# Moving the start of the split-weight tiles by 0, 32, 64 or 96 bytes from one tile to the next

## The chip, the cores and the metric

The kernel runs on one core of one Trainium2 chip. The metric is the device time of one execution in microseconds; 2619.27 us is the median of three runs of the kernel before (2615.98 to 2622.2). The profiled execution, from which all rows below come, took 2616.97 us; its span from the first to the last instruction is 2614.9 us.

## The reference

One hybrid decoder layer for 512 tokens of width 2048, in float32. Cut to what matters here:

```
n1   = rms_norm(x);  proj = n1 @ w_in                      # 2048 x (1024 + 3072 + 1024 + 16 + 4096)
y_pool = causal_pool_mixer(...);  o = gated_delta_rule(...)  # 8 heads, chunks along the sequence
merged = sigmoid(gate_pool) * (y_pool @ w_up_pool) + sigmoid(gate_dn) * (y_dn @ w_up_dn)
h    = x + merged @ w_out                                  # 2048 x 2048
h    = h + hierarchical_moe(rms_norm(h))                   # 32 experts, top 2 of one group
h    = h + sigmoid(rms_norm(h) @ w_ple_gate) * (p @ w_ple_proj)   # w_ple_gate 2048 x 2048
out  = rms_norm(h)
```

The large products outside the experts (w_in, w_up_pool, w_up_dn, w_out, w_ple_gate) are what the change is about.

## The kernel before, in words

**The split.** A large product is made of three passes in the format fp32r. Each operand is split in two: a high part (`hi`, ScalarE casts it, line 94) and a low part (`lo` = raw minus high, VectorE, line 95). `mm3` (lines 97 to 101) then issues three matmuls into the same PSUM bank: high by high (L99), and the two mixed products (L100, L101). A profile shows for each of them a MATMUL on PE (the moving operand streams through, 512 or 256 columns) and an LDWEIGHTS on PEld (the stationary operand, 128 columns, loaded while the matmul before it runs). A row names the tiles in the order moving, stationary.

**Weights in the mixer.** `load_w` (L322) brings 512 KB of a weight by DMA into `raw` (three buffers), splits it into `whi` and `wlo` (two buffers each), and one such tile feeds 24 matmuls (`proj`, L373: four slices of the contraction, two halves of the columns, three passes). There the weight slice is stationary and the activations (`n1h`, `n1l`; later `yd`, `yh`, `yl`) move. `next_w` (L358) asks for the next tile when it hands one out, so ScalarE and VectorE split one tile ahead. The first four weight tiles are split elsewhere, into `fhi` and `flo` (L241), with 256 moving columns, and the 16 columns of beta and alpha into `ba_h` and `ba_l` (`gates_ba`, L489).

**Output projection.** In `project_out` (L879) it is the other way round: the weights of w_out (`whi`, `wlo`, 512 columns) move, and 128-column slices of the split activations `mh` and `ml` (three buffers each, `parts`, L886) are stationary. A weight tile again feeds 24 matmuls, an activation tile 12. While the last block runs, `h` is transposed for the router (L915 copies the result, L919 multiplies by the router's weights).

**Tail.** The gate of the per-layer embedding: `gate_weights` (L1523) splits w_ple_gate into `whi` and `wlo` of a second pool (four buffers each); they move, with 512 columns in three blocks and 256 in the last two (`tail`, L1532), and slices of `xh` and `xl` are stationary.

The experts between output projection and tail multiply whole float32 tiles (`wm` by `xe`, `hmT`) with 64 stationary columns, and a few fp32r tiles of their own (`G` by `ghi`, `yhi` by `GT`).

**Where the tiles lie.** A pool lays the buffers of its tiles end to end in each partition. In the built program the starts of the fp32r operands are these, modulo 256 bytes (slices of an operand start at multiples of 512 bytes from there, those of `ba_h` and `ba_l` at multiples of 64):

| product | moving starts at | stationary starts at |
|---|---|---|
| mixer (n1, yd, yh, d by whi, wlo) | 224 | 224 |
| first tiles (n1 by fhi, flo) | 224 | 64 |
| beta and alpha (n1 by ba_h, ba_l) | 224 | 64, 128, 192, 0 in turn |
| output projection (whi, wlo by mh, ml) | 224 | 224 |
| tail (whi, wlo by xh, xl) | 160 | 128 |

**What sets the order.** Instructions are recorded as the code runs and put in order by a scheduler, per engine; in the norm and the experts TensorE's order (in the norm ScalarE's and VectorE's too) is the one in which the code is written. Each engine runs its own list in order.

Of the kernel before, what the change touches and what calls it, by code (L numbers as in the profile page):

```python
# [10 lines left out]
F32R = mybir.dt.float32r  # L11
# [6 lines left out]
P = 128  # L18
T = 512
# [43 lines left out]
class Layer:  # L63
    def __init__(self, ctx, tc, a, dbg=None):
        self.ctx, self.tc, self.nc, self.a, self.dbg = ctx, tc, tc.nc, a, dbg or {}
        self.consts = ctx.enter_context(tc.tile_pool(name="consts", bufs=1))
        self.psum = ctx.enter_context(tc.tile_pool(name="psum", bufs=4, space=bass.MemoryType.PSUM))

# [250 lines left out]
            self.xs.append(x)  # L319


    def load_w(self, src, width):  # L322
        nc = self.nc
        raw = self.p_w.tile([P, 1024], F32, name="raw", bufs=3)
        hi = self.p_w.tile([P, 1024], F32R, name="whi", bufs=2)
        lo = self.p_w.tile([P, 1024], F32R, name="wlo", bufs=2)
        r = raw.rearrange("p (k c) -> p k c", c=width)
        nc.sync.dma_start(r, src)
        self.last_split = self.split(hi, lo, raw)
        return hi.rearrange("p (k c) -> p k c", c=width), lo.rearrange("p (k c) -> p k c", c=width)  # L330
# [548 lines left out]
    def project_out(self, pp):  # L879
        nc, a = self.nc, self.a  # L880
        for t in range(NT):
            nc.scalar.dma_start(self.h[:, t, :], a["x"][0, t * P:(t + 1) * P, :])
        self.pl = self.bank("dl")
        self.ss2 = self.p_rt.tile([P, NT, 4], F32, name="ss2", bufs=1)

        def parts():  # L886
            for k in 4 * list(range(KD)):
                h = pp.tile([P, T], F32R, name="mh", bufs=3)
                l = pp.tile([P, T], F32R, name="ml", bufs=3)
                self.split(h, l, self.m[k])  # L890
                yield h, l

        parts = parts()
        ready = [next(parts)]
        for i, (c0, w) in enumerate(((0, 512), (512, 512), (1024, 512), (1536, 512))):
            cs = slice(c0, c0 + w)
            ps = [self.bank("mm") for _ in range(NT)]
            n = 1024 // w
            for k0 in range(0, KD, n):
                hi, lo = self.next_w()  # L900
                for k in range(n):
                    ready.append(next(parts, None))
                    mh, ml = ready.pop(0)
                    for t in range(NT):
                        s = slice(t * P, (t + 1) * P)
                        self.mm3(ps[t][:, 0:w], mh[:, s], ml[:, s], hi[:, k, :], lo[:, k, :],
                                 start=k0 + k == 0, stop=k0 + k == KD - 1)
            for t in range(NT):
                d = self.h[:, t, cs]
                nc.vector.scalar_tensor_tensor(d, ps[t][:, 0:w], 0.5, d, op0=OP.mult, op1=OP.add)  # L910
            for k in range(c0 // P, (c0 + w) // P):
                f = pp.tile([P, T], F32, name="hT", bufs=2)
                pt = self.h_transposed(k)
                if k % 2:
                    nc.vector.tensor_copy(f, pt)  # L915
                else:
                    nc.scalar.copy(f, pt)
                o = 64 * (k % 2)
                nc.tensor.matmul(self.pl[o:o + 36, :], self.wr[:, k, :], f, start=k < 2, stop=k >= KD - 2)  # L919
            for t in range(NT):  # L920
                j = pp.tile([P, T], BF16, name="sqj", bufs=1)
                nc.scalar.activation(j[:, 0:w], self.h[:, t, cs], AF.Square, accum_out=self.ss2[:, t, i:i + 1])
# [600 lines left out]
    def gate_weights(self, w):  # L1523

        raw = self.next_weights().rearrange("p k c -> p (k c)")
        for i in range(2):
            hi = self.p_w.tile([P, 1024], F32R, name="whi", bufs=4)
            lo = self.p_w.tile([P, 1024], F32R, name="wlo", bufs=4)
            self.split(hi, lo, raw[:, 1024 * i:1024 * i + 1024])
            yield hi.rearrange("p (k c) -> p k c", c=w), lo.rearrange("p (k c) -> p k c", c=w)  # L1530

# [175 lines left out]
```

## Time and profile before

| | us |
|---|---|
| median of 3 runs | 2619.27 |
| profiled execution | 2616.97 |
| its span | 2614.9 |
| PE busy in the span | 2511.0 |
| ScalarE (ACT) busy | 776.7 |
| VectorE (DVE) busy | 1148.9 |

The profile shows one execution. PE's busy time is that of pipelined matmuls and overlaps itself: a matmul of 512 columns is shown with some 390 ns, though the next one starts some 227 ns after it. What a matmul costs in a dense stretch is therefore read from the starts of successive matmuls in the timeline (start in us with two decimals), over as many as stand in one stretch. The granted clock of TensorE is 0.992 of full speed over the span; the mixer, the output projection's stretches cited below and the tail's cited stretches stand at 1.00, which is the 2.4 GHz level.

### The profile page before, as it was taken

The numbers are of one execution on the slowest core, as the hardware profiler recorded it, in microseconds if no ns is written. First come the engines' busy times: TensorE is split into PE (matmuls) and PEld (weight loads), VectorE is DVE, ScalarE is ACT, GpSimd is POOL, SyncE is SP. The second block draws the span as 40 slices with busy tenths as digits, with TensorE's granted clock in tenths as the row PEclk, the third lists the DMA queues.
The fourth block names the chain that finished last, engine by engine and source line by source line (L and its number), as shares of the span: only waits on it lengthen the run. The fifth ranks groups of instructions, "written<-read, shape, count | busy, mean of one in ns | idle before, by whom it ended". The sixth has DMA issues, their size and how long they took to land. (4 is left out here: it accounts for less than half of the span.)

```text
span 2614.9 us, 30940 instructions
## 1 busy us (share of the span) xinstructions
PE 2511.0 (96%) x12358; PEld 1720.5 (66%) x12358; DVE 1148.9 (44%) x2042; ACT 776.7 (30%) x1308; POOL 83.8 (3%) x92
## 2 busy tenths in 40 slices
PE   7999999999999999999989899999999999989998
PEld 6788888887888888877754444444444444444788
DVE  6475766765222233345453343333334333315435
ACT  4233242424222222234434222223222222113323
POOL 1001110100000000000000000000000000000001
PEclk9999999999999999999989999999999999999999
DMA  5222223234333333373237799999999999977222
GB/s 153 81 79 73 79 58 94 68 97 125 97 97 97 97 97 97 97 292 126 81 138 283 324 378 416 379 422 374 422 377 421 384 421 376 401 307 278 97 97 97
DMA packets 197975, 554.16 MB, mean 212 GB/s; under 512 B 30378, under 2 KB 127043, under 8 KB 148035
## 3 DMA queue, kind: packets, MB, share of 16 engines
q1 hardware_dynamic: 194610, 543.61, 55.4%
q10 hardware_dynamic: 2640, 4.33, 0.5%
q0 software_dynamic: 576, 4.19, 0.4%
q8 instruction: 99, 1.62, 0.2%
q14 instruction: 50, 0.40, 0.0%
HBM read 545.01 MB, written 7.08 MB: 211 GB/s over the span
## 5 line engine op out<-in xcount | busy, mean ns | idle before, releaser
L1138 PE MATMUL ps_mm<-wm,xe 128*64 128x512 f32 x2048 | 454.7, 597 | 10.6 <-DMA wm<-in_w_gate_dram 5.3
L99 PE MATMUL ps_mm<-n1h,whi 128*128 128x512 f32 x1120 | 450.4, 402 | 0.9 <-ACT whi L94 0.9
L101 PE MATMUL ps_mm<-n1h,wlo 128*128 128x512 f32 x1120 | 437.3, 391 | 1.7 <-DVE wlo L95 1.6
L100 PE MATMUL ps_mm<-n1l,whi 128*128 128x512 f32 x1120 | 437.1, 390 | 0.0
L95 DVE TENSOR_TENSOR wlo<-raw,whi 128x1024 fp32r<-128x1024 f32 x206 | 254.4, 1235 | 412.5 <-ACT whi L94 401.4
L94 ACT CAST whi<-raw 128x1024 fp32r<-128x1024 f32 x206 | 216.3, 1050 | 545.1 <-PE ps_mm L100 538.9
L1138 PEld LDWEIGHTS ps_mm<-wm,xe 128*64 128x64 f32 x2048 | 141.8, 137 | 287.0 <-issue 264.1
L95 DVE TENSOR_TENSOR glo<-h,ghi 128x512 fp32r<-128x512 f32 x128 | 137.2, 1096 | 361.1 <-ACT ghi L94 352.8
L94 ACT CAST ghi<-h 128x512 fp32r<-128x512 f32 x128 | 139.6, 1134 | 425.3 <-PE ps_dl L1113 314.2
L101 PEld LDWEIGHTS ps_mm<-n1h,wlo 128*128 128x128 f32 x1120 | 210.0, 188 | 47.3 <-DVE wlo L95 2.5
L99 PEld LDWEIGHTS ps_mm<-n1h,whi 128*128 128x128 f32 x1120 | 210.8, 188 | 40.3 <-ACT whi L94 1.3
L100 PEld LDWEIGHTS ps_mm<-n1l,whi 128*128 128x128 f32 x1120 | 210.9, 188 | 38.7
L1197 PE MATMUL ps_mm<-wm,hmT 128*64 128x512 f32 x960 | 218.8, 601 | 9.0 <-DVE eidx L1353 6.9
L1221 DVE TENSOR_TENSOR h<-h,ps_dl 128x512 f32<-128x512 f32 x256 | 160.2, 682 | 98.7 <-PE ps_dl L1219 95.9
L1197 PEld LDWEIGHTS ps_mm<-wm,hmT 128*64 128x64 f32 x960 | 66.5, 137 | 135.2 <-issue 130.0
L1113 PE MATMUL ps_dl<-G,ghi 128*128 128x256 f32 x512 | 134.2, 298 | 1.9 <-DVE G L1092 0.9
L1114 PE MATMUL ps_dl<-G,glo 128*128 128x256 f32 x512 | 128.5, 288 | 5.2 <-DVE glo L95 5.2
L1113 PEld LDWEIGHTS ps_dl<-G,ghi 128*128 128x128 f32 x512 | 99.2, 194 | 42.4 <-issue 38.9
L1218 PE MATMUL ps_dl<-yhi,GT 128*128 128x512 f32 x256 | 107.8, 421 | 14.0 <-ACT xe L1120 14.0
L1114 PEld LDWEIGHTS ps_dl<-G,glo 128*128 128x128 f32 x512 | 99.2, 194 | 7.1 <-DVE glo L95 6.9
L101 PE MATMUL ps_mm<-whi,ml 128*128 128x512 f32 x256 | 100.0, 391 | 2.1 <-DVE ml L95 2.1
L1219 PE MATMUL ps_dl<-ylo,GT 128*128 128x512 f32 x256 | 100.7, 393 | 0.0
(402 smaller groups left out, 3262.4 us busy)
## 6 DMA issues: line engine op xcount, KB each, us to landing
wm<-in_w_gate_dram SPq DMA_DIRECT2D x128, 1024.0 KB, 8.7
wm<-in_w_up_dram SPq DMA_DIRECT2D x128, 1024.0 KB, 10.2
wm<-in_w_down_dram SPq DMA_DIRECT2D x128, 1024.0 KB, 9.5
raw<-in_w_in_dram SPq DMA_DIRECT2D x144, 512.0 KB, 3.7
raw<-in_w_out_dram SPq DMA_DIRECT2D x32, 512.0 KB, 3.7
wm<-in_w_ple_gate_dram SPq DMA_DIRECT2D x16, 1024.0 KB, 5.0
raw<-in_w_up_dn_dram SPq DMA_DIRECT2D x16, 512.0 KB, 3.5
raw<-in_w_up_pool_dram SPq DMA_DIRECT2D x16, 512.0 KB, 3.6
```

The costliest lines, as they stand in the source:

```text
L94: i = self.nc.scalar.copy(hi, src)
L95: return i, self.nc.vector.tensor_tensor(lo, src, hi.bitcast(F32), op=OP.subtract)
L99: mm(ps, whi, xhi, start=start, stop=False)
L100: mm(ps, whi, xlo, start=False, stop=False)
L101: mm(ps, wlo, xhi, start=False, stop=stop)
L1113: nc.tensor.matmul(p, hi[:, t, :], Gf[:, t, :], start=t == 0, stop=False)
L1114: nc.tensor.matmul(p, lo[:, t, :], Gf[:, t, :], start=False, stop=t == NT - 1)
L1138: nc.tensor.matmul(ps[64 * i:64 * i + 64, :], xe[k][:, c0 + 64 * i:c0 + 64 * i + 64], ws[i][:, j, :], start=k == 0, stop=k == KD - 1)
L1197: nc.tensor.matmul(out[cb][64 * i:64 * i + 64, :], hT[:, k, 64 * i:64 * i + 64], ws[i][:, cb * T:(cb + 1) * T], start=k == 0, stop=k == 3)
L1218: nc.tensor.matmul(pc, GT[:, s], yh, start=True, stop=False)
L1219: nc.tensor.matmul(pc, GT[:, s], yl, start=False, stop=True)
L1221: nc.vector.tensor_tensor(d, d, pc, op=OP.add)
```

## The change

A helper `shifted` counts the tiles made under a name, allocates each 32 elements (128 bytes per partition) longer, and returns a view that begins 8 elements (32 bytes) further on after each full turn of the name's buffers: 0, 32, 64, 96 bytes, then 0 again. `whi`, `wlo`, `mh` and `ml` are taken from it; `raw`, the activations, `xh`, `xl` and everything else stay as they are.

```diff
+        self.turns = {}
...
+    def shifted(self, pool, name, n, bufs):
+
+        i = self.turns[name] = self.turns.get(name, -1) + 1
+        t = pool.tile([P, n + 32], F32R, name=name, bufs=bufs)
+        o = 8 * (i // bufs % 4)
+        return t[:, o:o + n]
+
     def load_w(self, src, width):
         nc = self.nc
         raw = self.p_w.tile([P, 1024], F32, name="raw", bufs=3)
-        hi = self.p_w.tile([P, 1024], F32R, name="whi", bufs=2)
-        lo = self.p_w.tile([P, 1024], F32R, name="wlo", bufs=2)
+        hi = self.shifted(self.p_w, "whi", 1024, 2)
+        lo = self.shifted(self.p_w, "wlo", 1024, 2)
...
             for k in 4 * list(range(KD)):
-                h = pp.tile([P, T], F32R, name="mh", bufs=3)
-                l = pp.tile([P, T], F32R, name="ml", bufs=3)
+                h = self.shifted(pp, "mh", T, 3)
+                l = self.shifted(pp, "ml", T, 3)
...
         for i in range(2):
-            hi = self.p_w.tile([P, 1024], F32R, name="whi", bufs=4)
-            lo = self.p_w.tile([P, 1024], F32R, name="wlo", bufs=4)
+            hi = self.shifted(self.p_w, "whi", 1024, 4)
+            lo = self.shifted(self.p_w, "wlo", 1024, 4)
```

Since each buffer is 128 bytes longer, the second buffer of a name also lies 128 bytes further on modulo 256. In the built program the stationary starts of the mixer are thus 224, 96, 0, 128, 32, 160, 64, 192 modulo 256 in turn, a new one with each tile, against a moving operand that stays at 224. In the output projection both operands take many pairs of starts; in the tail the moving one takes all eight multiples of 32 and the stationary one stays at 128.

The order of the instructions is the same on PE, ACT, POOL and SP. On DVE two instructions move, at the end of the output projection, where the last copies for the router (hT) meet the router's root of the mean square (rs2s, rsq_j, rsq_b) and a small constant (turn). DVE there in the kernel before:

```order
L910 SCALAR_TENSOR_TENSOR h<-ps_mm,h 128x512 x4
L915 COPY hT<-ps_dl 128x512
L935 TENSOR_REDUCE rs2s<-ss_8854 128x4
L936 TENSOR_SCALAR rs2s<-rs2s 128x4
L81 TENSOR_SCALAR rsq_j_10309<-rs2s 128x4
L84 TENSOR_TENSOR rsq_b_10310<-rsq_j_10309 128x4
```

In the changed kernel, where all lines below the helper are eight further on, the same place on DVE reads:

```order
L918 SCALAR_TENSOR_TENSOR h<-ps_mm,h 128x512 x4
L923 COPY hT<-ps_dl 128x512 x2
L943 TENSOR_REDUCE rs2s<-ss_8854 128x4
L1357 MEMSET turn 128x1
L944 TENSOR_SCALAR rs2s<-rs2s 128x4
L82 TENSOR_SCALAR rsq_j_10309<-rs2s 128x4
```

The last copy of hT, which stood after the seventh small instruction of the root, now stands ahead of all of them, and the constant `turn`, which stood behind the root, now stands behind its first instruction.

## Rows read from the trace of the kernel before

**Rows 1.** The page's busy times: busy us, share of the span, instructions.

```profile
PE 2511.0 (96%) x12358; PEld 1720.5 (66%) x12358; DVE 1148.9 (44%) x2042; ACT 776.7 (30%) x1308; POOL 83.8 (3%) x92
```

**Rows 2.** Groups: line, engine, op, out<-moving,stationary, count | busy us, mean ns | idle before.

```profile
L99 PE MATMUL ps_mm<-n1h,whi 128*128 128x512 f32 x1120 | 450.4, 402 | 0.9 <-ACT whi L94 0.9
L95 DVE TENSOR_TENSOR wlo<-raw,whi 128x1024 fp32r<-128x1024 f32 x206 | 254.4, 1235 | 412.5 <-ACT whi L94 401.4
L94 ACT CAST whi<-raw 128x1024 fp32r<-128x1024 f32 x206 | 216.3, 1050 | 545.1 <-PE ps_mm L100 538.9
L101 PE MATMUL ps_mm<-whi,ml 128*128 128x512 f32 x256 | 100.0, 391 | 2.1 <-DVE ml L95 2.1
L99 PE MATMUL ps_mm<-whi,xh 128*128 128x512 f32 x128 | 51.4, 401 | 0.0
L99 PE MATMUL ps_mm<-yd,whi 128*128 128x512 f32 x128 | 49.8, 389 | 0.0
L99 PE MATMUL ps_dl<-whi,xh 128*128 128x256 f32 x128 | 35.7, 279 | 0.0
L99 PE MATMUL ps_dl<-whi,xh 128*128 128x512 f32 x64 | 25.3, 395 | 0.0
```

**Rows 3.** Timeline of PE, output projection, 16 starts: start us, us, instruction.

```profile
1156.14 0.39 PE L100 MATMUL ps_mm<-wlo,mh 128*128 128x512 f32 x1
...
1159.54 0.39 PE L100 MATMUL ps_mm<-wlo,mh 128*128 128x512 f32 x1
```

**Rows 4.** Timeline of PE, tail with 512 columns, 12 starts.

```profile
2456.22 0.39 PE L101 MATMUL ps_mm<-whi,xl 128*128 128x512 f32 x1
...
2458.79 0.40 PE L100 MATMUL ps_mm<-wlo,xh 128*128 128x512 f32 x1
```

**Rows 5.** Timeline of PE, beta and alpha, 13 starts.

```profile
56.69 0.39 PE L99 MATMUL ps_mm<-n1h,ba_h 128*16 128x512 f32 x1
...
59.44 0.39 PE L99 MATMUL ps_mm<-n1h,whi 128*128 128x512 f32 x1
```

**Rows 6.** Tile ba_h: duration ns min/median/max, first and last start us.

```profile
L100 PE MATMUL ps_mm<-n1l,ba_h x16: 389/396/397, 56.9 to 71.3; 128*16 128x512 f32 x16
```

**Rows 7.** Timeline of PE, first tiles with 256 columns, 17 starts.

```profile
47.96 0.28 PE L99 MATMUL ps_mm<-n1h,fhi 128*128 128x256 f32 x1
...
49.88 0.28 PE L100 MATMUL ps_mm<-n1l,fhi 128*128 128x256 f32 x1
```

**Rows 8.** Timeline of PE, tail with 256 columns, 20 starts.

```profile
2576.74 0.28 PE L101 MATMUL ps_dl<-whi,xl 128*128 128x256 f32 x1
...
2578.95 0.28 PE L99 MATMUL ps_dl<-whi,xh 128*128 128x256 f32 x1
```

**Rows 9.** Timeline of PE, mixer after a pause: 5 starts, then 12 more.

```profile
649.59 0.39 PE L99 MATMUL ps_mm<-n1h,whi 128*128 128x512 f32 x1
...
650.51 0.39 PE L100 MATMUL ps_dl<-d,whi 128*128 128x512 f32 x1
...
653.23 0.39 PE L101 MATMUL ps_dl<-dh,wlo 128*128 128x512 f32 x1
```

**Rows 10.** Chain of waits, an expert's float32 passes: start us, us, what.

```profile
2352.70 7.02 PE ps_mm L1138 x32
2359.72 0.43 PE ps_dl L99
```

**Rows 11.** Timeline of DVE, end of the output projection; idle before in brackets.

```profile
1338.92 0.16 DVE L935 TENSOR_REDUCE rs2s<-ss 128x4 f32<-128x16 f32 x1
...
1340.97 0.69 DVE L915 COPY hT<-ps_dl 128x512 f32<-128x512 f32 x1 [0.31 <-PE ps_dl L927]
...
1342.07 0.06 DVE L1349 MEMSET turn<- 128x1 f32 x1
...
1345.41 0.31 DVE L958 TENSOR_TENSOR lg<-l 128x144 f32<-128x144 f32 x1 [2.09 <-ACT l L947]
```

## The prediction

> **What bounds the kernel now.** I read the page's busy times first, then the groups, then the timeline of PE in the stretches that the change touches. PE is busy for 96% of the span [rows 1], and the splits that feed it wait for it, not it for them: ACT's casts of weights stood idle 538.9 us behind PE, DVE's subtractions 401.4 us behind those casts, while PE waited 0.9 us in 1120 matmuls of L99 [rows 2]. So a nanosecond on each fp32r matmul is a nanosecond of the kernel, and one on a split is hidden.
>
> The groups show how many matmuls have an operand whose start changes. Mixer: 1120 for each of the three passes with n1 (3360), 128 for each with yd and as many with yh (768), and 48 in the pool mix (16 calls of `mm3`, L444): 4176. Output projection: 256 for each pass, 768. Tail: 128 and 64 for each pass with 512 columns, 576; 128 for each with 256 columns, 384 [rows 2].
>
> What one of them costs I take from successive starts, since durations overlap. Output projection: 15 steps in 1159.54 - 1156.14 = 3.40 us, 226.7 ns [rows 3]. The mixer, once settled, has the same: 12 steps in 2.72 us, 226.7 ns [rows 9]. The tail, at the same shapes and with nothing to wait for, needs more: 11 steps in 2.57 us, 233.6 ns [rows 4]. Between them the code differs in no instruction and no size; what differs is where the operands lie: 224 against 224 modulo 256 in the first two, 160 against 128 in the tail (table of starts above). That makes the start address a suspect, and this change moves start addresses and hardly anything else.
>
> **A trial of the suspect that the kernel makes by itself.** The gates' small product has n1 moving from 224 and a stationary slice that steps by 64 bytes, so it goes through four starts in turn. Its 12 steps take 59.44 - 56.69 = 2.75 us, 229.2 ns [rows 5], and one and the same pass, L100, lasts 389 ns in some and 397 ns in others of its 16 matmuls [rows 6]. Aligned it would have been 226.7. The load there has 16 columns, not 128, so it is the nearest row for a start that rotates and no proof for the size.
>
> **The change part by part.**
>
> Mixer: seven of eight tiles no longer start where the moving operand does, modulo 256. Bounds for the mean step: from above the tail's 233.6, from below the float32 passes of the experts, which stand at 7.02 us for 32, 219.4 ns, at 64 stationary columns [rows 10]; nothing excludes that some distances are better than an equal start. I take 229.2, because it is the only row in which the start rotates: 4176 x (229.2 - 226.7) = 4176 x 2.5 ns = +10.4 us. The bounds for seven eighths of 4176 (3654): +3654 x 6.9 = +25.2 us, and -3654 x 7.3 = -26.7 us.
>
> Output projection: both operands rotate, each on its own count, so nearly every pair of starts occurs. Same value: 768 x 2.5 ns = +1.9 us; bounds for 672 of them +4.6 and -4.9 us.
>
> Tail, 512 columns: here the rotation may help. From 233.6 to 229.2 for 576: -2.5 us; bounds 0 and, at 219.4 for seven of eight, 504 x 14.2 = -7.2 us.
>
> Tail, 256 columns: here the distance of 32 bytes was not the dear one. 19 steps take 2.21 us, 116.3 ns [rows 8], while the first tiles of the mixer (224 against 64) need 1.92 us for 16, 120.0 ns [rows 7]. Half way: 384 x 1.8 = +0.7 us; bounds 0 and +1.4 us.
>
> Settling: after a pause the mixer's first four steps take 0.92 us, 230 ns each, before 226.7 sets in [rows 9]. If each of the 206 weight tiles [rows 2] brought such a stretch, that were 206 x 4 x 3.3 ns = 2.7 us. The gates' product changes its start in every third matmul, so its 229.2 holds that cost already; I add nothing and keep 0 to 2.7 us for the range.
>
> Splits: casts of 1050 ns and subtractions of 1235 ns [rows 2] write and read at other starts. If each became 10% longer, 206 x 0.1 us would lie on ACT and DVE, under the waits of 538.9 and 401.4 us named above: 0. Bounds: 0 either way while that cover stands.
>
> DVE's two moved instructions: the last copy of hT waits for PE, at 1340.97 [rows 11], and now holds up the ten small instructions of the root, which began at 1338.92. Seven of them, some 0.2 us each, go behind it, so the root is ready some 1.4 us later than 1342.07. What waits for it is DVE's own work up to L958, which came at 1345.41 after 2.09 us of idling for ACT: the cover is longer than the delay. 0; without the cover +1.4 us.
>
> Sum: 10.4 + 1.9 - 2.5 + 0.7 = +10.5 us. Against the profiled execution's 2616.97 us (2614.9 of span and 2.1 around it) that is 2627.5 us. The median of the runs is 2.3 us above the profiled one, so I forecast 2630 us.
>
> **A rule that speaks for no change.** The Trainium skill, "TensorE: Matmul & The Clock Gate", section "Step-by-step: what each phase is for", says that PE has two independent read ports into SBUF and that loading the next tile's weights takes nothing from the running matmul; "SBUF — State Buffer", section "Who interferes with whom", says that PE never waits on anyone. By that rule the start of an operand could not matter and the time would stay. The two durations of one pass [rows 6] speak against it; that the first tiles, 96 bytes from their moving operand, hold a steady 120.0 ns [rows 7] speaks somewhat for it.
>
> **The rivals.**
>
> No change. The tail's extra 6.9 ns come from something else, or 128-column loads settle whatever the distance, as the first tiles do [rows 7]. Then nothing moves but the tail, by at most 576 x 6.9 = -4.0 us (if its start was the cause after all): 2615 to 2619 us, with 2619 the likelier. For it: rows 7 and the rule above. Against: rows 4 to 6.
>
> Faster. The 226.7 of equal starts is itself a collision of the load with the stream, and other distances avoid part of it. Place: the mixer's stationary slices. The experts' passes show that 219.4 is to be had [rows 10], and the 256 columns of the tail, 32 bytes apart, are faster than the first tiles at 96 [rows 8, 7]. If a quarter of the mixer's and output projection's matmuls lost one step of 6.9 ns: 4944 / 4 x 6.9 = -8.5 us, with the tail at 226.7 -4.0 us: 2607 us. It decides once the mean step in the mixer is under 226.7 - 5.2 / 4.944 = 225.6 ns. Against it: the two unequal 512-column rows [rows 4, 5] are both above 226.7.
>
> Slower to the full. Every unequal start pays what the tail pays: +25.2 + 4.6 + 1.4 + 2.7 for settling = +34 us, 2653 us. Against it: the shorter durations in rows 6, at unequal starts too.
>
> **How the numbers follow.** About 0.2% (5.2 us) is what a measurement of this kernel can tell from no change. Forecast 42%, full 10%: both over 2624.5, so slower 52%. No change 28%. Faster 20%. The range for 8 in 10 leaves out half of the faster case and most of the full one: 2606 to 2651. The forecast's own range, with mixer steps of 228.2 to 231.2 ns (+-1.5 ns on 4944, +-7.4 us), is 2623 to 2637.
>
> **What would show it.** In the mixer's timeline the starts of successive matmuls should stand 229 ns apart in the mean instead of 226.7, and L99 to L101 should show durations that mix 389 with 397 ns, tile by tile of 24 matmuls. The tail's step should fall below 233.6. Steps of 226.7 in all mixer tiles would make the prediction wrong towards no change, steps under 225.6 towards faster, and a gain or loss of over 5 us outside mixer, output projection and tail would mean that I looked in the wrong place.

## The result, and the profile after

The changed kernel took 2638.74 us in the median of three runs (2636.9 to 2641.4) against 2619.27 us: 1.0076 times the time before, 95% interval 1.0052 to 1.01, so 19.5 us slower. The profiled execution took 2636.9 us, its span 2634.8 us.

The page's busy times, beside [rows 1]: PE is busy for 23.3 us more, PEld for 3.1, the other engines for no more than before.

```profile
PE 2534.3 (96%) x12358; PEld 1723.6 (65%) x12358; DVE 1148.6 (44%) x2042; ACT 775.9 (29%) x1308; POOL 83.8 (3%) x92
```

The groups that answer to [rows 2] (the helper shifted these lines by one: L100 to L102 are the three passes, L95 and L96 the splits):

```profile
L100 PE MATMUL ps_mm<-n1h,whi 128*128 128x512 f32 x1120 | 454.9, 406 | 0.9 <-ACT whi L95 0.9
L102 PE MATMUL ps_mm<-whi,ml 128*128 128x512 f32 x256 | 102.0, 398 | 2.1 <-DVE ml L96 2.1
L100 PE MATMUL ps_mm<-yd,whi 128*128 128x512 f32 x128 | 50.4, 394 | 0.0
L95 ACT CAST whi<-raw 128x1024 fp32r<-128x1024 f32 x206 | 215.7, 1047 | 557.5 <-PE ps_mm L101 551.0 <-DVE tu L738 5.4 <-PE ps_dl L101 0.9
L96 DVE TENSOR_TENSOR wlo<-raw,whi 128x1024 fp32r<-128x1024 f32 x206 | 254.2, 1234 | 426.5 <-ACT whi L95 403.7 <-PE ps_dl L772 20.8 <-PE ps_dl L589 1.6
```

The same work with the same waits: PE still waits 0.9 us for the splits, a cast still takes 1047 ns and a subtraction 1234 ns. The matmuls themselves are longer: 406, 398 and 394 ns against 402, 391 and 389. Where they cost the kernel its time is read from the first matmul of each stage. The timeline of PE in the kernel before (first matmul with yd, of the output projection, of the experts, of the tail with 512 and with 256 columns):

```profile
630.37 0.39 PE L99 MATMUL ps_mm<-yd,whi 128*128 128x512 f32 x1
...
1143.28 0.39 PE L99 MATMUL ps_mm<-whi,mh 128*128 128x512 f32 x1
...
1354.25 0.55 PE L1113 MATMUL ps_dl<-G,ghi 128*128 128x256 f32 x1 [0.94 <-DVE G L1092]
...
2416.75 0.50 PE L99 MATMUL ps_mm<-whi,xh 128*128 128x512 f32 x1
...
2559.35 0.28 PE L99 MATMUL ps_dl<-whi,xh 128*128 128x256 f32 x1
```

The same five in the changed kernel:

```profile
633.07 0.39 PE L100 MATMUL ps_mm<-yd,whi 128*128 128x512 f32 x1
...
1158.07 0.40 PE L100 MATMUL ps_mm<-whi,mh 128*128 128x512 f32 x1
...
1374.45 0.55 PE L1121 MATMUL ps_dl<-G,ghi 128*128 128x256 f32 x1 [0.94 <-DVE G L1100]
...
2436.75 0.50 PE L100 MATMUL ps_mm<-whi,xh 128*128 128x512 f32 x1
...
2578.69 0.28 PE L100 MATMUL ps_dl<-whi,xh 128*128 128x256 f32 x1
```

The differences, stage by stage: +2.7 us up to yd, +12.1 in the dense rest of the mixer (512.91 to 525.00 us), +5.4 in the output projection, -0.2 in the experts, -0.7 and +0.6 in the tail's two parts. Their sum is 19.9 us, the whole difference of the spans.

The dense rest of the mixer shows the cause tile by tile. First matmul of nine successive weight tiles (timeline of PE, changed kernel); 24 matmuls lie between two rows:

```profile
901.97 0.39 PE L100 MATMUL ps_mm<-n1h,whi 128*128 128x512 f32 x1
...
907.41 0.40 PE L100 MATMUL ps_mm<-n1h,whi 128*128 128x512 f32 x1
...
913.00 0.40 PE L100 MATMUL ps_mm<-yh,whi 128*128 128x512 f32 x1
...
918.60 0.40 PE L100 MATMUL ps_mm<-yh,whi 128*128 128x512 f32 x1
...
924.19 0.40 PE L100 MATMUL ps_mm<-n1h,whi 128*128 128x512 f32 x1
...
929.79 0.40 PE L100 MATMUL ps_mm<-n1h,whi 128*128 128x512 f32 x1
...
935.30 0.39 PE L100 MATMUL ps_mm<-n1h,whi 128*128 128x512 f32 x1
...
940.92 0.39 PE L100 MATMUL ps_mm<-n1h,whi 128*128 128x512 f32 x1
...
946.52 0.39 PE L100 MATMUL ps_mm<-yh,whi 128*128 128x512 f32 x1
```

In the built program these eight tiles start 0, 128, 32, 160, 64, 192, 96 and 224 bytes past the moving operand, modulo 256 (the *distance* below). They take 5.44, 5.59, 5.60, 5.59, 5.60, 5.51, 5.62 and 5.60 us: 226.7 ns a matmul at distance 0, 229.6 at 192, 232.9 to 234.2 at the others. Over the whole mixer (all steps from the start of one of its matmuls to the next start on PE, up to 245 ns) the means are:

| distance | 0 | 32 | 64 | 96 | 128 | 160 | 192 | 224 |
|---|---|---|---|---|---|---|---|---|
| ns per matmul | 227.4 | 233.2 | 233.3 | 233.8 | 232.6 | 233.5 | 230.1 | 233.1 |

The mean is 232.09 ns, against 227.60 before. It hides two stages: up to yd, among the small matmuls of the delta rule, the mean goes from 228.8 to 232.2 ns, behind it from 226.7 to 232.0.

Output projection, 16 starts, beside [rows 3]: 15 steps in 3.48 us, 232.0 ns.

```profile
1171.32 0.39 PE L101 MATMUL ps_mm<-wlo,mh 128*128 128x512 f32 x1
...
1174.80 0.40 PE L101 MATMUL ps_mm<-wlo,mh 128*128 128x512 f32 x1
```

Tail with 512 columns, beside [rows 4]: two tiles of 24 matmuls, the first at distance 0 (5.46 us, 227.5 ns), the second at 96 (5.63 us, 234.6 ns). Here too only some of the tiles got shorter; over the 576 matmuls the mean went from 233.33 to 232.15 ns.

```profile
2450.55 0.39 PE L100 MATMUL ps_mm<-whi,xh 128*128 128x512 f32 x1
...
2456.01 0.40 PE L100 MATMUL ps_mm<-whi,xh 128*128 128x512 f32 x1
...
2550.74 0.40 PE L100 MATMUL ps_mm<-whi,xh 128*128 128x512 f32 x1
...
2556.37 0.39 PE L100 MATMUL ps_mm<-whi,xh 128*128 128x512 f32 x1
```

DVE at the end of the output projection, beside [rows 11]: the last copy of hT stands ahead of the root now, and L966 (L958 before) still comes 4.44 us after that copy, as before. Its idle time shrank from 2.09 to 0.27 us: the cover held.

```profile
1361.17 0.69 DVE L923 COPY hT<-ps_dl 128x512 f32<-128x512 f32 x1 [1.91 <-PE ps_dl L935]
1361.78 0.16 DVE L943 TENSOR_REDUCE rs2s<-ss 128x4 f32<-128x16 f32 x1
...
1365.61 0.31 DVE L966 TENSOR_TENSOR lg<-l 128x144 f32<-128x144 f32 x1 [0.27 <-ACT l L955]
```

### The profile page after: what moved, and what is told of

Its sections match the earlier page's. It is cut to its first block, busy times and chain, and to the rows that moved or that the text cites. A ratio compares the mean times of both kernels' runs of the same rounds, so it can differ in the third digit from the quotient of the medians.

```text
span 2634.8 us, 30941 instructions
## 1 busy us (share of the span) xinstructions
PE 2534.3 (96%) x12358; PEld 1723.6 (65%) x12358; DVE 1148.6 (44%) x2042; ACT 775.9 (29%) x1308; POOL 83.8 (3%) x92
## 5 line engine op out<-in xcount | busy, mean ns | idle before, releaser
L100 PE MATMUL ps_mm<-n1h,whi 128*128 128x512 f32 x1120 | 454.9, 406 | 0.9 <-ACT whi L95 0.9
L102 PE MATMUL ps_mm<-n1h,wlo 128*128 128x512 f32 x1120 | 441.7, 395 | 1.1 <-DVE wlo L96 1.1
L101 PE MATMUL ps_mm<-n1l,whi 128*128 128x512 f32 x1120 | 441.4, 394 | 0.0
L96 DVE TENSOR_TENSOR wlo<-raw,whi 128x1024 fp32r<-128x1024 f32 x206 | 254.2, 1234 | 426.5 <-ACT whi L95 403.7
L95 ACT CAST whi<-raw 128x1024 fp32r<-128x1024 f32 x206 | 215.7, 1047 | 557.5 <-PE ps_mm L101 551.0
L96 DVE TENSOR_TENSOR glo<-h,ghi 128x512 fp32r<-128x512 f32 x128 | 136.9, 1094 | 361.4 <-ACT ghi L95 354.3
L95 ACT CAST ghi<-h 128x512 fp32r<-128x512 f32 x128 | 139.6, 1134 | 425.3 <-PE ps_dl L1121 314.3
L102 PEld LDWEIGHTS ps_mm<-n1h,wlo 128*128 128x128 f32 x1120 | 210.2, 188 | 51.3 <-DVE wlo L96 2.0
L100 PEld LDWEIGHTS ps_mm<-n1h,whi 128*128 128x128 f32 x1120 | 211.0, 188 | 44.2 <-ACT whi L95 1.3
L101 PEld LDWEIGHTS ps_mm<-n1l,whi 128*128 128x128 f32 x1120 | 211.1, 188 | 42.6
L102 PE MATMUL ps_mm<-whi,ml 128*128 128x512 f32 x256 | 102.0, 398 | 2.1 <-DVE ml L96 2.1
L101 PE MATMUL ps_mm<-wlo,mh 128*128 128x512 f32 x256 | 102.1, 399 | 0.0
```

Source lines behind the costliest of these rows:

```text
L95: i = self.nc.scalar.copy(hi, src)
L96: return i, self.nc.vector.tensor_tensor(lo, src, hi.bitcast(F32), op=OP.subtract)
L100: mm(ps, whi, xhi, start=start, stop=False)
L101: mm(ps, whi, xlo, start=False, stop=False)
L102: mm(ps, wlo, xhi, start=False, stop=stop)
```

## The experiments

The first four ask what it is about the starts that costs: the distance between the two operands (theory D), the change from tile to tile (C), or where the stationary operand lies by itself (S).

**All mixer weights 32 bytes further on, for good.** One small tile is put at the beginning of the weight pool:

```diff
+        self.p_w.tile([P, 8], F32, name="pad", bufs=1)
```

> The kernel before with one 32-byte pad ahead of the weight buffers, so that all weight tiles of the mixer start 32 bytes further on, always the same; yd, yh, mh, ml and d lie behind them and move along, n1 stays. Distance (stationary start minus moving start, modulo 256) is 32 in the 3360 matmuls on n1 and 0 in the rest of mixer and output projection; the tail is as before. Theory D (the distance sets the step): steps of 233.2 ns on n1 as in the changed kernel's tiles at 32, first matmul of the output projection 12 to 20 us later than 1143.3, total 2632 to 2640. Rival C (what costs is that the start changes from tile to tile): 2619, steps of 226.7. Rival S (the stationary operand's own start counts, whatever moves): as D on n1, and the yd, yh and mh stretches also above 226.7, total some 2640.

Measured: 2633.54 us, ratio 1.0045 (1.0028 to 1.0061). Groups of this run:

```profile
L99 PE MATMUL ps_mm<-n1h,whi 128*128 128x512 f32 x1120 | 455.9, 407 | 0.9 <-ACT whi L94 0.9
L100 PE MATMUL ps_mm<-yd,whi 128*128 128x512 f32 x128 | 49.9, 390 | 0.0
```

The output projection begins at 1156.53 us. Against n1 the distance is 32 throughout, and a matmul costs 233.1 ns; yd and yh moved with the weights, their distance is 0, and they cost 227.2. Nothing changes from tile to tile here, so C falls; the weights of yd start at the same addresses as those of n1, so S falls.

**n1 moved along.** The same, and 56 elements of padding in n1's pool, which restore distance 0 with every operand elsewhere:

```diff
+        self.p_n1.tile([P, 56], F32, name="n1pad", bufs=1)
```

> The kernel of e1_weights_32 with n1 also moved, by a pad of 224 bytes below it, to the same start modulo 256 as the weights: distance 0 again, both starts other than in the kernel before. D: steps of 226.7, total 2619 within 4 us. S: steps and total as in e1_weights_32. C: 2619.

Measured: 2619.62 us, ratio 0.9994 (0.9984 to 1.0003); mixer steps of 227.55 ns, output projection from 1143.96 us.

```profile
L99 PE MATMUL ps_mm<-n1h,whi 128*128 128x512 f32 x1120 | 450.3, 402 | 0.9 <-ACT whi L94 0.9
```

Modulo 256 the weights lie where they lay in the run before, and the cost is gone: the distance is the cause.

**A turn of 256 bytes.** The changed kernel's helper with a step of 256 bytes, for whi of the mixer and output projection alone (all others plain):

```diff
-        o = 8 * (i // bufs % 4)
+        o = 64 * (i // bufs % 2)
```

> The changed kernel's helper on the high weight tiles of mixer and output projection alone, with a shift of 0 or 256 bytes in turn every two tiles; the distance modulo 256 stays 0. D with a period of 256 bytes: 226.7 ns, 2619 within 4 us. C: the start changes every 48 matmuls, half as often as in the changed kernel, so up to half its loss, 2624 to 2629. If the period is longer than 256 bytes: steps above 226.7 in the shifted tiles.

Measured: 2621.56 us, ratio 0.9997 (0.9987 to 1.0007); 227.57 ns.

```profile
L100 PE MATMUL ps_mm<-n1h,whi 128*128 128x512 f32 x1120 | 450.5, 402 | 0.9 <-ACT whi L95 0.9
```

A start that moves by 256 bytes costs nothing, nor does the helper; for the step, 256 bytes on is the same place.

**A finer map.** Steps of 8 bytes, for the weights of mixer and output projection alone:

```diff
-        o = 8 * (i // bufs % 4)
+        o = 2 * (i // bufs % 16)
```

> The changed kernel's helper on the weight tiles of mixer and output projection alone (mh, ml and the tail as before), with 16 shifts of 0 to 120 bytes in steps of 8; with the buffers 128 bytes apart that gives 32 distances, some 130 matmuls each. D: a step for every distance; at multiples of 32 bytes those of the changed kernel (0: 227, 192: 230, others 232.6 to 233.8), total 2630 to 2645. It shows whether any distance is under 226.7. C: about the changed kernel's loss at every distance alike.

Measured in one run: 2642.62 us, mixer 231.99 ns, output projection from 1159.38 us. The cheapest distances are 0 (227.9 ns), 120 (228.0), 240 (228.3) and 192 (228.8), the dearest 96 (234.2). None beats 0, so for 512 columns the mixer and the output projection of the kernel before stood at the best start already.

**The mixer's part undone.** The changed kernel with plain tiles in `load_w`:

```diff
-        hi = self.shifted(self.p_w, "whi", 1024, 2)
-        lo = self.shifted(self.p_w, "wlo", 1024, 2)
+        hi = self.p_w.tile([P, 1024], F32R, name="whi", bufs=2)
+        lo = self.p_w.tile([P, 1024], F32R, name="wlo", bufs=2)
```

> One part of the change undone: the mixer's and the output projection's weight tiles (whi, wlo of load_w) are plain again, so that every start there is 224 against 224 in the mixer; the activations mh and ml and the tail's weights still rotate as in the changed kernel. Theory D (a matmul of 512 columns pays for an unequal start, modulo 256, of its moving and its stationary operand): mixer steps back at 227.5 ns, output projection begins near 1143 us instead of 1158, its own steps stay near 232 (768 x 5 = +4 us), tail about 0; 2624 us, ratio 1.0015 to 1.002. Rival P (the cost comes from the longer buffers, or from anything that the change moves besides starts in the mixer): the mixer stays slow, 2636 to 2639 us, ratio 1.007. Rival E (equal starts in the output projection matter less since both operands rotate): 2619 to 2621 us, ratio 1.000.

Measured: 2625.21 us, ratio 1.0013 (1.0004 to 1.0023). The first matmul of the output projection, from the timeline of PE:

```profile
1143.34 0.39 PE L100 MATMUL ps_mm<-whi,mh 128*128 128x512 f32 x1
```

and its group:

```profile
L100 PE MATMUL ps_mm<-whi,mh 128*128 128x512 f32 x256 | 102.0, 399 | 0.0
```

The mixer is back to the 0.1 us; the output projection, where only mh and ml still rotate, keeps its 232.27 ns and ends 5.3 us late (first matmul of the experts at 1359.58 us instead of 1354.25). The two parts are separate, and D gave both; of the 5.3 us about 1.5 are not the starts' (see the output projection below).

**The tail put right.** The kernel before with the tail's tiles 64 elements longer and read from element 56 (512 columns: distance 0) or 40 (256 columns: distance 64, the shortest seen after the change, 113.5 ns):

```diff
+            o = 56 if w == T else 40
-            hi = self.p_w.tile([P, 1024], F32R, name="whi", bufs=4)
+            hi = self.p_w.tile([P, 1024 + 64], F32R, name="whi", bufs=4)[:, o:o + 1024]
...
```

> The kernel before with only the tail's weight tiles moved within longer buffers: in the blocks of 512 columns the moving operand starts where the stationary one does (modulo 256), in the blocks of 256 columns 64 bytes before it. Theory D: 512-column steps from 233.3 to 227.4 ns (576 x 5.9 = -3.4 us), 256-column steps from 116.7 to 113.5 (384 x 3.2 = -1.2 us); about -4.6 us, ratio 0.998 to 0.9985. Rival (what the tail pays comes from something else than its starts): steps stay at 233 and 117, ratio 1.000. Rival (the tail's weights arrive or are split too late for a faster PE): steps fall as in D, but PE waits, and the total falls by less than 2 us, ratio over 0.999.

Measured: 2619.03 us, ratio 0.9991 (0.9982 to 1.0). Timeline of PE, 12 starts as in [rows 4]:

```profile
2461.16 0.39 PE L101 MATMUL ps_mm<-whi,xl 128*128 128x512 f32 x1
...
2463.65 0.39 PE L100 MATMUL ps_mm<-wlo,xh 128*128 128x512 f32 x1
```

11 steps in 2.49 us, 226.4 ns: what [rows 4] paid above 226.7 was its start. The whole tail takes 194.8 us instead of 198.1. The total fell by only 2.0 us (0.9991, where D gave 0.998 to 0.9985), but not in the third rival's way: PE waits 3.4 us in the tail in both kernels. Where the other 1.3 us went I have not followed. With 256 columns D failed: 117.8 ns instead of 113.5, and longer than the 116.7 of before. So the same distance of 64 gives 113.5 ns among tiles that rotate and 117.8 among tiles that don't: at 256 columns distance alone does not set the step. The padded run with two blocks, further down, whose tail is that of the kernel before at the same starts, shows 117.8 there too instead of 116.7.

**The experts' gathering products too.** As in the run before, and `ghi` and `glo` moved by 64 bytes:

```diff
-            hi = pp.tile([P, NT, P], F32R, name="ghi", bufs=2)
-            lo = pp.tile([P, NT, P], F32R, name="glo", bufs=2)
+            hi, lo = (pp.tile([P, NT * P + 64], F32R, name=nm, bufs=2)[:, 16:16 + NT * P]
+                      .rearrange("p (t c) -> p t c", t=NT) for nm in ("ghi", "glo"))
```

> As the run before, and the experts' gathering products (G by ghi and glo, 256 columns, 1024 matmuls) get a distance of 64 bytes too. Theory D: their step from 119.3 to 113.5 ns where PE does not wait; 1024 x 5.8 = 5.9 us if PE sets the time there, which gives -10.5 us with the tail, ratio 0.996. Rival W (the experts' stretch is set by the weights' transfers, whose queues are busy for 97% of it): PE waits longer instead, the stretch keeps its length, and the total is that of the run before, -4.6 us, ratio 0.998.

Measured: 2617.43 us, ratio 0.9987 (0.9978 to 0.9996). Groups of the kernel before, then of this run:

```profile
L1113 PE MATMUL ps_dl<-G,ghi 128*128 128x256 f32 x512 | 134.2, 298 | 1.9 <-DVE G L1092 0.9 <-ACT ghi L94 0.2
```

```profile
L1113 PE MATMUL ps_dl<-G,ghi 128*128 128x256 f32 x512 | 131.2, 295 | 2.1 <-DVE G L1092 0.9 <-ACT ghi L94 0.6
```

The steps did get shorter, from 119.3 to 116.1 ns in the mean over ghi and glo (steps of up to 130 ns), which is 3.3 us in 1024, not the 5.9 of theory D. The time from the first of them to the tail hardly shows it: 1061.9 us here, 1062.3 to 1066.6 in the kernel before, the changed one and the runs above, where the experts are the same and their start alone differs. Cut in two at a point behind the last gathering matmul, it does. The columns are window, its length, busy us and count of PE, PEld, DVE, ACT and POOL, granted clock, share of the DMA engines, GB/s. The kernel before, then this run:

```profile
1354.25:2309.55 955.30, 918.33 (x4577) 434.97 (x4577) 356.70 (x526) 253.67 (x364) 0.17 (x1) 0.99 0.92 377
2309.55:2416.75 107.20, 97.25 (x439) 45.05 (x438) 36.49 (x62) 30.07 (x59) 0.00 (x0) 0.95 0.78 304
```

```profile
1356.02:2308.49 952.47, 915.13 (x4577) 431.79 (x4577) 356.49 (x526) 252.56 (x364) 0.16 (x1) 0.99 0.92 378
2308.49:2417.96 109.47, 99.51 (x438) 45.59 (x438) 36.49 (x62) 30.05 (x59) 0.00 (x0) 0.94 0.76 298
```

The same 4577 matmuls take 952.5 us here, 955.3 before and 955.3 to 957.1 in all other runs. So 2.8 us of the shorter steps did reach the path, and rival W, by which the stretch keeps its length, fell. The part behind the cut took back 2.3 of them: the granted clock is 0.51 from 2351.1 to 2354.5 us here, where the kernel before stands at 1.00 (2337 to 2360 us). What lowers it there the runs don't show. The total is 3.6 us under the kernel before, where D gave 10.5. This is the only version with an interval wholly below 1, and it is within the 0.2% that count as no change here.

**One pass in three at distance 32.** The kernel before with the small tile between whi and wlo, so that against n1 whi stays at distance 0 and wlo lies at 32.

```diff
         hi = self.p_w.tile([P, 1024], F32R, name="whi", bufs=2)
+        self.p_w.tile([P, 8], F32, name="pad", bufs=1)
         lo = self.p_w.tile([P, 1024], F32R, name="wlo", bufs=2)
```

> The kernel before with 32 bytes put between whi and wlo in the mixer: against n1, whi keeps an equal start and wlo lies 32 bytes on; against yd and yh whi lies 32 bytes before and wlo is equal. One pass in three with n1 (1120) and two in three with yd and yh (512) have an unequal start. Theory D, the distance counts for the loaded operand: 1632 x 5.8 = +9.5 us of matmul time, of which the mixer's waits take up some; output projection begins near 1151 us. D1: it is the load of the next tile into PE while the matmul before it streams that pays, so the long step stands between the matmul ahead of L101 or L100 with wlo and that matmul. D2: the matmul that uses wlo pays, so the long step stands behind it. Rival S (all steps of a run of matmuls get longer once any start differs): 3360 x 5.8, as in the run with all weights 32 bytes on, output projection begins at 1156 us.

Measured in one run: 2641.88 us, output projection from 1160.79 us. Not +9.5 us but more than with every pass at 32. The timeline of PE, four successive starts of the mixer:

```profile
999.92 0.40 PE L99 MATMUL ps_mm<-n1h,whi 128*128 128x512 f32 x1
1000.16 0.40 PE L100 MATMUL ps_mm<-n1l,whi 128*128 128x512 f32 x1
1000.40 0.39 PE L101 MATMUL ps_mm<-n1h,wlo 128*128 128x512 f32 x1
1000.62 0.40 PE L99 MATMUL ps_mm<-n1h,whi 128*128 128x512 f32 x1
```

The three steps are 0.24, 0.24 and 0.22 us, 233 in the mean. Over the mixer's matmuls on n1, L99 takes 232.1 ns, L100, which streams while wlo is loaded, 237.1, and L101 228.6. The pass that meets the unequal load is the longest (D1 in that point), but L99, which has no unequal start on either side, is long as well. My sum, which gave each pair of operands its own price, is wrong; the rival that expected every step to be long came nearest. Nor had I seen that mh lies 32 bytes from whi in this run: its output projection takes 215.45 us instead of 210.97.

**The same starts, two blocks.** Two readings were left: one unequal load keeps its neighbours from their steady pace (R), or every change of the stationary start costs (C). `proj` issues a tile's 16 matmuls with whi first and its 8 with wlo after them:

```diff
-                    self.mm3(ps[c], hi[:, k, s], lo[:, k, s], xh[k0 + k], xl[k0 + k],
...
+                    mm(ps[c], hi[:, k, s], xh[k0 + k], start=k0 + k == 0, stop=False)
+                    mm(ps[c], hi[:, k, s], xl[k0 + k], start=False, stop=False)
+                if k == 3:
+                    for j in range(4):
+                        for c in range(2):
+                            mm(ps[c], lo[:, j, c * P:(c + 1) * P], xh[k0 + j],
...
```

> The kernel of the run before with 32 bytes between whi and wlo, but in the mixer's projections each weight tile's 24 matmuls are issued in two blocks: 16 with whi, then 8 with wlo (before: whi, whi, wlo in turn). The same matmuls meet the same starts. Theory R (at an equal start the matmuls fall into a steady rhythm of 226.7 ns after some five steps, and one other start in three keeps them from it): against n1, the block with whi settles at 226.7 to 229 ns and the block with wlo at 233; mean step 229 to 230.5 instead of 232.8, output projection begins at 1148 to 1153 us instead of 1160.8; total 2628 to 2634 us. Rival C (each change of the stationary start from one matmul to the next costs by itself): two changes in 24 instead of 16, steps of 226.7 in both blocks, output projection begins at 1144 to 1146 us. Rival S (once whi and wlo start differently every step of the mixer is long): 232.8, 1160 us.

Its control is the same order without the pad:

> Control for the run with two blocks: the kernel before with that order and no moved start. All theories: the order alone costs nothing, steps of 227 to 228 ns, output projection begins at 1143 to 1145 us, 2619 to 2623 us, ratio 1.000. If the order itself costs or gains, the run beside it is to be read against this one.

Measured: 2643.77 us, ratio 1.008 (1.0063 to 1.0097), and for the control 2627.09 us, 1.0025 (1.0015 to 1.0035). The control's 5.4 us were not expected: its mixer begins yd at 636.47 us instead of 630.37, while the dense rest takes 512.56 us as before (512.91). The order costs in the stage of the delta rule. Part of it is TensorE's clock: in the control the granted clock is 0.50 from 421.9 to 425.3 us and from 613.1 to 616.5 us, each time soon after PE had waited some 2 us (2.20 for Tm, 1.95 for vr), and 1.00 in the kernel before from 415 to 425 and from 610 to 620 us. Half of these 6.8 us, 3.4 us, is my estimate of what that costs; the rest I have not followed. In the dense rest the order costs nothing, so the two are compared there. Timeline of PE with the pad, a block of whi, a block of wlo (its eight matmuls in one row), the next tile:

```profile
1005.20 0.39 PE L384 MATMUL ps_mm<-n1h,whi 128*128 128x512 f32 x1
...
1008.38 0.39 PE L384 MATMUL ps_mm<-n1h,whi 128*128 128x512 f32 x1
...
1008.84 2.02 PE L389 MATMUL ps_mm<-n1h,wlo 128*128 128x512 f32 x8
1010.70 0.39 PE L384 MATMUL ps_mm<-n1h,whi 128*128 128x512 f32 x1
```

The control:

```profile
1005.78 1.98 PE L388 MATMUL ps_mm<-n1h,wlo 128*128 128x512 f32 x8
1007.59 0.39 PE L383 MATMUL ps_mm<-yh,whi 128*128 128x512 f32 x1
```

With the pad, 14 steps of whi take 3.18 us (227.1 ns each) and the eight of wlo 1.86 us (232.5); in the control the eight take 1.81 us (226.3). The matmuls at distance 0 are back at their pace though they meet the very operands of the run before. From yd to the output projection this run needs 520.82 us, 8.3 more than its control; with the passes in turn it was 527.39, 14.5 more than the kernel before. The mean step over the mixer, 230.6 ns, is just above what R expected. The total and the output projection's first matmul, at 1159.94 us, missed R's ranges (2628 to 2634 us, 1148 to 1153 us): R had not counted what the order costs before yd, 6.1 us in the control and 8.75 here, where the granted clock is 0.50 in three stretches instead of two, nor the output projection's unequal starts. Both rivals fell, since steps in the block of wlo are long without any change of start, and whi's are short.

## Why the prediction was right in its direction and short in its size

The forecast was 2630 us in a range of 2606 to 2651; 2638.74 us were measured, +19.5 us instead of +10.5.

**PE sets the time, splits are hidden.** Right: no wait for a split grew, and the stages add up to the difference of the spans.

**Starts are the cause.** Right. Rows 4 to 6 were read as a trial of the start; the runs with the weights moved alone, and with n1 moved along, show it. With the loaded operand 32 bytes on, a matmul costs 233.1 ns instead of 227.2. The Trainium skill, "TensorE: Matmul & The Clock Gate", section "Step-by-step: what each phase is for", has PE read both operands through ports of their own, so that a load takes nothing from the matmul that runs; by that rule the start could not matter, and the trace does not agree, though no run shows the ports themselves.

**Mixer, +10.4 us.** This step failed: "I take 229.2, because it is the only row in which the start rotates". The mean step became 232.09 ns, so 4176 x (232.09 - 227.60) = 18.7 us instead of 10.4. [rows 5] stand at distances 96, 160, 224 and 32, which with 128 columns cost 233.1 to 233.8; in that stretch they cost 229. Rotation as such was no reason to take a lower price: a fixed distance of 32 costs 233.1 ns, one among rotating tiles 233.2. Whether the load of 16 columns made that row cheap, or its four starts in turn, no run separates. [rows 4], a load of 128 columns at an unequal start, had the right price. I had written that the row is no proof for the size and kept its value all the same.

**All of it on the path.** A second, smaller miss the other way: of the 18.7 us only 14.8 reached the output projection. 1920 of the 4176 matmuls stand before yd, among the small matmuls of the delta rule. There a step was 228.8 ns already and became 232.2, so they cost 1920 x 3.4 = 6.5 us, and yd begins 2.7 us later. Of the 3.8 us between, 3.3 show as idle time of PE that went (10.9 us between 51 and 630 us before, 7.6 between 51 and 633 after). The 2256 behind it cost 12.1 us, 5.4 ns each, all of it on the path.

**Output projection, +1.9 us.** The same failed step: 226.98 to 232.48 ns, 768 x 5.5 = 4.2 us by its steps; 5.4 us passed. The rest is no work of the starts but of TensorE's clock (columns as above):

```profile
1162.10:1165.50 3.40, 3.40 (x10) 2.63 (x9) 1.70 (x3) 0.62 (x1) 0.00 (x0) 0.50 1.00 422
```

The granted clock is at its 1.2 GHz level for these 3.4 us, after PE had waited 2.1 us for ml, and eight steps take 423 to 427 ns, some 1.5 us more than at 232. The kernel before has the same wait and stays at 1.00. The run with n1 moved along has the fall too, with steps of 226.98 ns, and its output projection takes 212.56 us instead of 210.97.

**Tail.** 512 columns: -2.5 us forecast, -0.7 measured, for the price was the same 229.2 and is 232.15. 256 columns: +0.7 forecast, +0.6 measured; with distance no full account there, half way between two rows was right by luck.

**Settling.** Adding nothing was right. In the dense rest twelve tiles at distance 0 come behind a tile at 224, and all their steps but the last stand at 226.5 to 226.8 ns in the mean, from the first one on. Steps of 228 to 230 ns at the head of such tiles stand only before yd, behind pauses and small matmuls, and the kernel before has them in the same places. At unequal starts no steady step follows.

**Splits and DVE's move, 0.** Right, by the durations and by the 4.44 us from the last copy to L966.

**The rivals.** "Slower to the full" had the better price (unequal starts pay 230.1 to 233.8 ns, mostly 233) and too high a total: it counted from 226.7 ns where the mixer's mean was 227.60, added 2.7 us for settling, and let the delta stage take up nothing. "Faster" fell with the map, in which no distance beats 0; "No change" with the first run, in which 32 bytes alone cost 12 us.

## What to carry to other kernels

Before padding or rotating a buffer that feeds dense fp32r matmuls, print the starts of the moving and the stationary operand modulo 256 bytes and see whether they agree: here, with 512 columns, an equal start was worth 5 to 6 ns in 227, and one pass in three with another start made all three longer. Take the price of a suspect from a row with the same load size, even if another row shows the movement better. Where small matmuls and waits stand between, count what PE's idle time takes up, and take the step before from that stretch, before putting a price on the path. And when two runs of the same instructions differ by 1 to 4 us, look at the granted clock stretch by stretch before calling it noise.

## What the runs showed of the hardware that was not expected

- With 512 columns the step depends on the distance with a period of 256 bytes: 227.4 ns at 0, 230.1 at 192, 232.6 to 233.8 at the other multiples of 32; 120 and 240 bytes (228.0, 228.3) are nearly as good as 0.
- Each distance has a rhythm of its own: behind yd at 0 every step is 226 to 227, at 32 steps of 231 to 232 and of 235 alternate, at 128 a step of 241 ns comes every seventh time.
- One unequal load in three makes even the matmul between two equal ones long (232.1 ns); in blocks of their own the equal ones return to 227 within a few steps.
- With 256 columns the distance does not decide alone: 64 bytes gave 113.5 ns in tiles that rotate, 117.8 in the tail's fixed ones and 116.1 in the gathering products; 224 bytes gave 116.7 in the kernel before and 117.8 in the padded run with two blocks.
- At the same wait, as at the head of the output projection, the granted clock fell to 0.50 in some runs and not in others; that fall cost some 1.5 us.

That the load's reads and the stream's reads meet in the memory would fit all of this; no run shows the reads, so the mechanism stays argued. Also open: the part of the two blocks' 6 us in the stage of the delta rule that the clock does not explain, and why the clock falls in some runs only.
